# A delta-rule loop written out as one fixed order on four engines, with a smaller state and a rewritten k eviction

## The chip, the cores and the metric

The kernel runs on one core of one Trainium2 chip. The metric is device time in microseconds (us). The kernel before took 1830.32 us in the median of 3 runs (1828.99 to 1832.56).

## The reference

A two-layer decoder trunk on 1024 tokens of width 1024, all in float32. Layer 0 mixes the tokens with RWKV-7's delta rule, layer 1 with differential attention; each is followed by a gated per-layer embedding (PLE), and a norm ends it. The part that the change touches is layer 0's mixer. For each of 16 heads, `k`, `r`, `v`, a decay `w` and a rate `a` come from projections, and the state (64 x 64 per head) runs through the tokens:

```
kk = (k * k_k) / norm ;  b = kk * a ;  k = k * (1 + (a - 1) * k_a)
def step(state, (r_t, w_t, k_t, v_t, kk_t, b_t)):
    sa    = state @ kk_t
    state = state * w_t - sa b_t^T + v_t k_t^T
    y_t   = state @ r_t
y = groupnorm(y) * ln_w + ln_b + sum(r * k * r_k) * v      # the sum is the "bonus"
h = x + (y * silu(gate)) @ w_out
```

## The kernel before

The sequence is cut into 16 chunks of 64 tokens (`for c in range(NCH)`). Products with the large weights are three fp32r matmuls of high and low parts each (lines 75 to 77, `mm3`); products of the recurrence are plain float32, and each of those shows as two records of the trace. The 16 heads stand in two groups `st` of 8, four pairs `p_` with two halves `h`; a pair fills 128 partitions.

A chunk is a chain. `chain_x` multiplies the state with the chunk's `kk` and `r` (line 855) and adds masked products with `v` (line 864); ScalarE copies the result `x` (line 878), and GpSimd multiplies the state by the chunk's decay into `spl` (line 875). `chain_u` multiplies by a triangular inverse (line 890), and VectorE scales it into `vu` (line 895). `chain_s` makes the state's addition (line 906), which VectorE adds to `spl` (line 910), and finishes the outputs (line 916), which ScalarE copies into `y` (line 923). In the state of before a pair's two 64 x 64 blocks lie on the diagonal of a 128 x 128 tile, with zeros beside them.

Beside the chain runs other work. For each group of the next chunk, `stage1` loads `kkr` and `kb`, multiplies `kb` by the decay on GpSimd (`kbp`, line 171), transposes it (line 175) into `kbn` (ScalarE, line 176), makes the mask products `pm` (line 185) and masks them on VectorE (line 188), and makes the bonus: two passes on GpSimd (lines 157 and 158), two transposes (line 162), two sums on VectorE (line 166). Each 128 tokens (two chunks) have their norm (`norm`, `norm2`, lines 953 to 970), a transpose of `y` (line 981, `turn`), a gating (line 984) with the split into `gh` on ScalarE (line 71) and `gl` on VectorE (line 72), and the output projection of 48 matmuls (`op`, `mms`), which VectorE adds to the residual (line 997). The first four chunks instead carry layer 1's PLE projections (`pps`) and the loading and splitting of the eight rows of the output weight (`wo_row`).

The order is made by the tile scheduler: the chain's matmuls stand under `high_priority`, the rest lies in lists (`later`, `ahead`) that `weave` mixes by cost and `fill` hands out in budgets between the steps of the chain. SyncE issues the loads.

Before the loop, `ev_k` (line 423 on) takes each of 16 pieces of the k projection out of PSUM and makes `k * (1 + (a - 1) k_a)`, `kk` and `b`, scaled by exponentials of the summed decay (`pinv`, `ep`); `kst` (line 464) transposes the squares of `kk` for its norm, one piece later.

Of the kernel before, what the change touches and what calls it, by code (L numbers as in the profile page):

```python
# [11 lines left out]
F32 = mybir.dt.float32  # L12
# [4 lines left out]
ALU = mybir.AluOpType  # L17
# [20 lines left out]
def trunk(ctx: ExitStack, tc: tile.TileContext, A, out):  # L38
    nc = tc.nc
    V, S, G, T = nc.vector, nc.scalar, nc.gpsimd, nc.tensor  # L40
# [95 lines left out]
    units = {}  # L136

    def stage1(st, c):
# [15 lines left out]

        def bonus():
            pr = early["co"].tile([P, 4, L], F32, tag="prod", name="pr" + u, bufs=1)
            G.tensor_tensor(out=pr, in0=kkr[:, :, oc], in1=kb[:, :, oc], op=ALU.mult)
            G.tensor_tensor(out=pr, in0=pr, in1=vec["r_k"][:, j0:j0 + 4].unsqueeze(2).to_broadcast([P, 4, L]),
                            op=ALU.mult)
            pt = ps1[0].tile([P, 2, P], F32, tag=ps1[1], name="prt" + u, bufs=2)  # L160
            for p_ in range(2):
                T.transpose(pt[:, p_], pr[:, 2 * p_:2 * p_ + 2].rearrange("p a l -> p (a l)"), ident)
            po = (c % 2) * 64
            bo = bon[po:po + 64, c // 2, st * 8:st * 8 + 8].rearrange("p (a b h) -> p a b h", a=2, b=2)
            for b in range(2):
# [12 lines left out]
        def mh():
# [12 lines left out]
        return [(load, 0), (turn, 430), (mh, 850), (bonus, 430)]  # L191

    with NB("ab") as ab, NP("psab") as pp:
# [12 lines left out]
        G.tensor_scalar(out=hka1, in0=vec["k_a"], scalar1=-0.5, scalar2=1.0, op0=ALU.mult, op1=ALU.add)  # L206
# [127 lines left out]
        with NB("cpool") as cpl:  # L334
# [82 lines left out]
            with NB("kr") as a3:  # L417
# [5 lines left out]
                def ev_k(j, hf, ps):  # L423
# [11 lines left out]
                    t = tmp(f"kt{j}{hf}")  # L435
# [380 lines left out]
    with NB("d") as d, NP("psco") as pp:  # L816
# [26 lines left out]
        def chain_x(c):  # L843
# [3 lines left out]
            if c + 1 < NCH:  # L847
                vload(c + 1)
# [786 lines left out]
```

## Time and profile before

| | |
|---|---|
| median of the runs | 1830.32 us |
| profiled execution | 1828.3 us |
| its span | 1826.5 us |
| TensorE busy | 1684.7 us, 92% of the span |
| VectorE busy | 1350.9 us, 74% |
| ScalarE busy | 760.4 us, 42% |
| GpSimd busy | 634.5 us, 35% |
| mean granted clock of TensorE | 0.963 |

The busy shares are means over stages with different limits. The chunks run from 588.2 us, where chunk 0's state product starts, to 911.2 us, where chunk 15's outputs have been copied: 323.0 us in all. Chunks 4, 6, 8, 10, 12 and 14 start at 666.7, 704.5, 745.2, 785.1, 829.7 and 868.8 us. The k eviction lies between 125 and 250 us.

### The profile page before, as it was taken

How to read it: one execution, taken by the hardware profiler on the slowest of the kernel's cores; microseconds unless marked ns; L12 is line 12 of the kernel's file. 1: busy time of each engine (PE TensorE's matmuls, PEld its weight loads, DVE VectorE, ACT ScalarE, POOL GpSimd, SP SyncE). 2: the span in 40 equal slices, each digit the busy share in tenths (PEclk: the TensorE clock that was granted, in tenths of full speed). 3: DMA queues.
4: the chain of work that ended last, by engine and by line, in shares of the span. 5: the costliest groups of instructions: out<-in, count | busy, mean ns of one | idle time of the engine just before them, and what ended most of it. 6: DMA issues, size and time to landing. Idle time of an engine off the chain costs nothing.

```text
span 1826.5 us, 30473 instructions
## 1 busy us (share of the span) xinstructions
PE 1684.7 (92%) x11320; PEld 1397.6 (77%) x11320; DVE 1350.9 (74%) x3083; ACT 760.4 (42%) x1594; POOL 634.5 (35%) x705
## 2 busy tenths in 40 slices
PE   6899999898897988898899999899999999999998
PEld 5677778887676877777678878788888888777786
DVE  7878954698994687666766747887877878856665
ACT  6566543346344332223333434444444444544332
POOL 4436644224324355455310333323323323311200
PEclk9999999998998989999999999999999999999999
DMA  7125444434225534444243411101101101431121
GB/s 267 41 61 166 129 106 109 125 102 119 73 67 186 186 127 127 122 129 131 97 172 128 132 51 39 54 7 56 56 7 56 53 10 56 154 99 34 58 93 69
DMA packets 164401, 175.97 MB, mean 96 GB/s; under 512 B 74845, under 2 KB 127837, under 8 KB 164254
## 3 DMA queue, kind: packets, MB, share of 16 engines
q1 hardware_dynamic: 161950, 169.84, 30.2%
q10 hardware_dynamic: 2304, 4.20, 0.6%
q8 instruction: 89, 1.46, 0.4%
q14 instruction: 58, 0.48, 0.1%
HBM read 124.19 MB, written 49.81 MB: 95 GB/s over the span
## 4 chain that ended last, share of the span: by engine, by line
PE 51%; DVE 10%; ACT 2%; issue 1%; DMA 0%; POOL 0%; ACTq 0%; DVEq 0%
PE qkv L75 6%; PE qkv L76 6%; PE qkv L77 6%; PE av L1359 3%; PE sc L1319 2%; PE sc L1320 2%; PE fg L75 2%; PE fg L76 2%; PE fg L77 2%; PE op L75 2%; PE op L77 2%; PE op L76 2%; PE do L75 1%; PE pg L76 1%; PE pg L77 1%; PE do L76 1%
## 5 line engine op out<-in xcount | busy, mean ns | idle before, releaser
L1329 ACT ACTIVATE e<-sc,mx 128x256 f32<-128x256 f32 (+7 forms) x128 | 94.0, 738 | 111.0 <-DVE mx L1326 60.0
L1273 POOL TENSOR_TENSOR rp<-rp,rq 128x128 f32<-128x128 f32 x64 | 34.8, 543 | 237.6 <-DVE rq L1268 189.7
L1359 PE MATMUL av<-vh,aT 128*128 128x128 f32 x576 | 81.1, 280 | 6.3 <-DVE aT L1355 6.3
L1359 PEld LDWEIGHTS av<-vh,aT 128*128 128x128 f32 x576 | 75.6, 195 | 12.8 <-DVE aT L1355 8.9
L1325 DVE TENSOR_REDUCE mxs<-sc 128x1 f32<-128x128 f32 (+6 forms) x112 | 74.2, 682 | 0.5
L1319 PE MATMUL sc<-k,q 128*128 128x512 f32 (+2 forms) x192 | 71.5, 379 | 2.2 <-ACT e L1329 2.2
L229 DVE SCALAR_TENSOR_TENSOR xmt<-hT,cB,xmt 128x512 f32<-128x512 f32 x64 | 63.5, 1012 | 6.6 <-ACT xmt L228 6.3
L1320 PE MATMUL sc<-k,q 128*128 128x512 f32 (+2 forms) x192 | 64.8, 348 | 0.0
L1361 ACT ACTIVATE o<-av,r 128x128 f32<-128x128 f32 x64 | 23.5, 367 | 88.4 <-PE av L1359 88.4
L875 POOL TENSOR_TENSOR spl<-state,plast 64x256 f32<-64x256 f32 x60 | 41.4, 690 | 49.6 <-DVE state L910 42.7
L1341 DVE SCALAR_TENSOR_TENSOR e<-e,r,e 128x128 f32<-128x128 f32 (+3 forms) x64 | 56.5, 883 | 1.2
L560 DVE TENSOR_TENSOR tb<-tb,tm 128x31 f32<-128x31 f32 (+15 forms) x124 | 53.9, 435 | 3.6
L558 DVE TENSOR_TENSOR tm<-tb,nb 128x31 f32<-128x31 f32 (+15 forms) x124 | 53.9, 434 | 3.6
L188 DVE TENSOR_TENSOR m<-pm,mmask 128x512 f32<-128x512 f32 x64 | 41.1, 682 | 20.0 <-PE pm L185 19.7
L1301 POOL CAST q<-q 64x128 fp32r<-64x128 f32 x128 | 38.5, 302 | 49.4 <-PE sc L1320 45.6
L1267 DVE TENSOR_TENSOR rp<-qkv,rc 128x256 f32<-128x256 f32 x64 | 27.1, 423 | 38.3 <-PE qkv L77 30.1
L1292 POOL CAST k<-k 64x256 fp32r<-64x256 f32 x64 | 26.1, 408 | 83.7 <-ACT k L1290 82.5
L185 PE MATMUL pm<-kkr,kb 64*128 64x128 f32 x512 | 50.8, 307 | 3.1 <-ACT kbn L176 2.2
L1355 DVE COPY aT<-at 128x512 f32<-128x512 f32 (+2 forms) x96 | 52.0, 550 | 1.1 <-PE at L1353 0.4
L185 PEld LDWEIGHTS pm<-kkr,kb 64*128 64x128 f32 x512 | 40.4, 203 | 12.9 <-issue 6.0
L1353 PE MATMUL at<-ident,e 128*128 128x128 f32 x288 | 47.4, 277 | 2.8 <-DVE e L1341 2.3
L923 ACT COPY y<-xy 64x512 f32<-64x512 f32 x32 | 18.6, 580 | 71.4 <-PE xy L916 71.0
(1180 smaller groups left out, 6001.5 us busy)
## 6 DMA issues: line engine op xcount, KB each, us to landing
pp_d<-ppo SPq DMA_DIRECT2D x32, 256.0 KB, 2.3
kb_d<-kb SPq DMA_DIRECT2D x16, 512.0 KB, 2.6
kkr<-kkr_d SPq DMA_DIRECT2D x32, 256.0 KB, 3.2
kb<-kb_d SPq DMA_DIRECT2D x32, 256.0 KB, 3.3
x<-in_x SPq DMA_DIRECT2D x8, 512.0 KB, 5.5
kkr_d<-ep SPq DMA_DIRECT2D x16, 256.0 KB, 2.6
kkr_d<-rt SPq DMA_DIRECT2D x16, 256.0 KB, 2.6
bb<-kb_d SPq DMA_DIRECT2D x32, 128.0 KB, 2.6
```

The lines of the kernel that those rows point to most:

```text
L75: T.matmul(ps, lhsT=ah, rhs=bh, start=start, stop=False)
L76: T.matmul(ps, lhsT=ah, rhs=bl, start=False, stop=False)
L77: T.matmul(ps, lhsT=al, rhs=bh, start=False, stop=stop)
L185: ms.append(T.matmul(pm[h][:, p_], lhsT=kb[hs, p_], rhs=kkr[hs, p_], start=True, stop=True))
L229: V.scalar_tensor_tensor(out=t, in0=hT[:, kt, half(hf)], scalar=cB[:, g, kt:kt + 1], in1=t, op0=ALU.mult, op1=ALU.add)
L558: V.tensor_tensor(out=tv, in0=tb[:, j:j + 1, 0:w].to_broadcast([P, n, w]), in1=nb[:, j + 1:32, j:j + 1].to_broadcast([P, n, w]), op=ALU.mult)
L1319: T.matmul(ps[:, b0:b1], lhsT=q1[:, m, ts_], rhs=k1[:, m, b0:b1], start=True, stop=False)
L1320: T.matmul(ps[:, b0:b1], lhsT=q0[i % 2][:, m], rhs=k2[:, b0:b1], start=False, stop=True)
L1325: V.tensor_reduce(out=seed, in_=ps[:, 0:n - P], axis=AX.X, op=ALU.min)
L1329: S.activation(e[:, 0:n], ps[:, 0:n], AF.Exp, scale=-1.0, bias=mx, accum_out=l_[:, m:m + 1])
L1341: V.scalar_tensor_tensor(out=es[0][:, 0:n], in0=es[1][:, 0:n], scalar=r[:, 1:2], in1=es[0][:, 0:n], op0=ALU.mult, op1=ALU.add)
L1359: T.matmul(po, lhsT=aT[kb // 4][:, kb % 4], rhs=c["vh"][:, kb], start=(kb == 0), stop=(kb == i))
```

## The change

In the loop every instruction of TensorE, VectorE, ScalarE and GpSimd keeps the order in which the code issues it (a wrapper calls `keep_in_program_order` while `pin` is set; SyncE's is left to the scheduler), and that order is written out, step by step, in the place of the lists and budgets. The steps of a tile are cut finer (`norm`, `squares`, `bonus_v`, `sums`, `roots`, `scaled`, `added`, `turn`, `turned`, `m0`, `m1`, `squares1`), and likewise those of `stage1`.

The state becomes one tile of 128 x 512 without the zero blocks. Its product takes 16 matmuls of 64 rows, 128 weight columns and 64 moving columns a chunk, in the place of 8 of 128 x 128 x 128; `spl` is one instruction on GpSimd in the place of four, and so is the state's sum on VectorE. The chain's `xy` is one tile of two PSUM banks.

The bonus multiplies `r * k` once on GpSimd and sums on TensorE, against a matrix `rk2` of two columns (8 matmuls a group), and two copies on ScalarE; the transposes and the sums on VectorE are gone. Of the masks one half stays on VectorE; the other is copied by ScalarE and then multiplied in place by GpSimd. In the k eviction VectorE has three passes in the place of five, ScalarE two more, GpSimd one less. The early gate rows are prepared at the end of chunk 13, and the last tiles' pieces (`t6`, `t7`) behind the loop stand in another order: all 48 projection matmuls of tile 6 now lie there, where 12 stood in chunk 15.

Counted over the program, VectorE goes from 3085 to 2912 instructions, ScalarE from 1363 to 1459, GpSimd from 710 to 652; the attention layer's order is the same.

```diff
+        def g(*a, **k):
+            r = f(*a, **k)
+            if self.pin:
+                tc.keep_in_program_order(r)
+            return r
...
-            for h in range(2):
-                V.tensor_tensor(out=m[:, h], in0=pm[h],
-                                in1=early["mmask"][:, st:st + 1].to_broadcast([P, 4, P]), op=ALU.mult)
+            mask = early["mmask"][:, st:st + 1].to_broadcast([P, 4, P])
+            S.copy(m[:, 1], pm[1])
+            G.tensor_tensor(out=m[:, 1], in0=m[:, 1], in1=mask, op=ALU.mult)
+            V.tensor_tensor(out=m[:, 0], in0=pm[0], in1=mask, op=ALU.mult)
...
+                    ms.append(T.matmul(pt[64 * s_:64 * s_ + 64, p_], lhsT=pr_[:, s_, p_],
+                                       rhs=early["rk2"][:, 4 * s_ + p_], start=True, stop=True))
...
-                    t = tmp(f"kt{j}{hf}")
-                    V.tensor_scalar(out=t, in0=a, scalar1=hka[:, jj], scalar2=hka1[:, jj],
-                                    op0=ALU.mult, op1=ALU.add)
-                    V.tensor_tensor(out=t, in0=ps3, in1=t, op=ALU.mult)
...
+                    V.tensor_tensor(out=q, in0=ps3, in1=pinv, op=ALU.mult)
...
+                    V.scalar_tensor_tensor(out=a, in0=a, scalar=1.0, in1=q, op0=ALU.add, op1=ALU.mult)
...
-                    V.tensor_scalar(out=a, in0=a, scalar1=-0.5, scalar2=-0.5, op0=ALU.mult, op1=ALU.add)
...
-                    V.tensor_tensor(out=kb[:, :, 1 - px], in0=t, in1=pinv, op=ALU.mult)
-                    V.tensor_tensor(out=a, in0=kk, in1=a, op=ALU.mult)
-                    G.tensor_tensor(out=kb[:, :, px], in0=a, in1=pinv, op=ALU.mult)
+                    S.activation(q, q, AF.Copy, scale=hka1[:, jj])
+                    V.scalar_tensor_tensor(out=kb[:, :, 1 - px], in0=a, scalar=hka[:, jj], in1=q,
+                                           op0=ALU.mult, op1=ALU.add)
+                    S.activation(kb[:, :, px], a, AF.Copy, scale=hkk[:, jj])
...
-                    ms += [T.matmul(px_[st][:, p_].rearrange("p h l -> p (h l)"), lhsT=kkr[:, p_],
-                                    rhs=state[st][:, p_], start=(p_ == 0), stop=False, skip_group_check=True)
-                           for p_ in range(4)]
+                            ms.append(T.matmul(px[:, h, st, p_], lhsT=kkr[half_(h), p_], rhs=state[half_(h), st, p_],
+                                               start=(st == 0 and p_ == 0), stop=False, skip_group_check=True))
...
+                V.tensor_tensor(out=state, in0=pS, in1=spl.rearrange("p (s j) l -> p s j l", s=2), op=ALU.add)
...
+            chain_x(c)
+            unit("decayed", 0)
+            if pj and not odd:
+                pj["turned"]()
+                pj["turn"](1)
...
+            more()
+            unit("mh", 0)
+            if pj and not odd:
+                pj["turned"]()
...
+            chain_u(c)
...
+            chain_s(c)
...
+            if c == 3:
+                more(9)
+                for kt in (2, 3, 6, 7):
+                    wo_row(kt)
...
+            more(2)
+            unit("turn", 1)
+            if w and odd:
+                w["added"]()
+                w["turn"](0)
+            more(9)
```

`unit` issues a step of `stage1` for the next chunk, `w` is the tile whose norm is under way, `pj` the one in projection, and `more` issues six projection matmuls at a time.

The first place is the start of an even chunk. On TensorE in chunk 6, between `x`'s products and the next, before (`ytr` is the transpose of `y`, `op` the projection, `u` the triangular product, `kbt` the transpose of `kbp`):

```order
L864 MATMUL xy_6_6867<-vu_6627,m_6_6621 64x64
L162 MATMUL prt_6_6839<-ident,pr_6_6836 128x128 x2
L981 MATMUL ytr_6844<-ident,y_5924 128x128 x4
L75 MATMUL op_6912<-rwo0h,gh_6783 128x512
L76 MATMUL op_6912<-rwo0l,gh_6783 128x512
L75 MATMUL op_7116<-rwo0h,gh_6783 128x512
L76 MATMUL op_7116<-rwo0l,gh_6783 128x512
L890 MATMUL u_6_6946<-x_6893,ti_2685 64x64
L175 MATMUL kbt_7_6906<-ident,kbp_7_6904 128x128 x4
```

and now (`pm` are the mask products of chunk 7):

```order
L50 MATMUL xy_6838<-vu_6616,m_6_6605 64x64
L50 MATMUL ytr_6880<-ident,y_5924 128x128 x4
L50 MATMUL op_6889<-rwo0h,gh_6800 128x512
L50 MATMUL op_6889<-rwo0l,gh_6800 128x512
L50 MATMUL op_6889<-rwo0h,gl_6801 128x512
L50 MATMUL op_6889<-rwo1h,gh_6800 128x512
L50 MATMUL op_6889<-rwo1l,gh_6800 128x512
L50 MATMUL op_6889<-rwo1h,gl_6801 128x512
L50 MATMUL pm_7_6897<-kkr_7_6823,kb_7_6824 128x128
L50 MATMUL pm_7_6896<-kkr_7_6823,kb_7_6824 128x128
```

The state and mask products that make `x` stand ahead of all these rows. Before, the products with `gl` (`op<-rwo0h,gl`) come only after `u`; now the third matmul behind the transpose needs it.

On ScalarE, which makes `gh`, from which VectorE makes `gl`, the same stretch in chunk 8 stood before as

```order
L957 ACTIVATE ysq_7491<-y_6855 128x1024
L71 ACTIVATE gh_7224<-sg_7042 128x512
L878 COPY x_7334<-xy_8_7313 64x512
L878 COPY x_7334<-xy_8_7308 64x512
L176 COPY kbn_9_7300<-kbt_9_7347 128x512
L71 ACTIVATE gh_7224<-sg_7042 128x512
L923 COPY y_7296<-xy_8_7313 64x512
L923 COPY y_7296<-xy_8_7308 64x512
L176 COPY kbn_9_7304<-kbt_9_7416 128x512
L1001 ACTIVATE h1sq_7634,ss_5440<-xr_7044 128x1024
```

and stands now as

```order
L50 COPY x_7312<-xy_7277 64x512 x2
L50 ACTIVATE gh_7239<-sg_6935 128x512
L50 COPY m_9_7264<-pm_9_7336 128x512
L50 ACTIVATE gh_7239<-sg_6935 128x512
L50 ACTIVATE h1sq_7350,ss_5430<-xr_6498 128x1024
L50 COPY kbn_9_7265<-kbt_9_7378 128x512
L50 COPY m_9_7268<-pm_9_7393 128x512
L50 COPY y_7261<-xy_7277 64x2x4x64 x2
L50 ACTIVATE ysq_7448<-y_6822 128x1024
L50 COPY kbn_9_7269<-kbt_9_7464 128x512
L50 COPY bon<-prt_9_7470 64x8 x2
```

The first `gh` was ahead of the copies of `x`; now it is behind them, and the copy of a mask half stands ahead of the second.

The second place is the end of an odd chunk, on VectorE. Before, around chunk 6 (`vu` the scaled triangular product, `m` the masks, `xr` the residual):

```order
L895 TENSOR_TENSOR vu_6627<-u_6_6946,rn 64x512
L966 TENSOR_TENSOR y_6414<-y_6414,gst_7046 128x1024
L895 TENSOR_TENSOR vu_6627<-u_6_6945,rn 64x512
L188 TENSOR_TENSOR m_7_6858<-pm_7_6920,mmask 128x512
L188 TENSOR_TENSOR m_7_6858<-pm_7_6919,mmask 128x512
L970 TENSOR_TENSOR y_6414<-y_6414,vn_7040 128x1024
L910 TENSOR_TENSOR state_5478<-s_6_6988,spl_6_6894 64x4x64 x2
L910 TENSOR_TENSOR state_5480<-s_6_6999,spl_6_6898 64x4x64 x2
L166 TENSOR_REDUCE bon<-prt_7_6940 64x2x2 x2
L997 TENSOR_TENSOR xr_6603<-op_6912,xr_6603 128x512
```

and now, at the end of chunk 5 and the start of chunk 6 (`sg` is the gating behind the transpose):

```order
L50 TENSOR_TENSOR m_6_6605<-pm_6_6678,mmask 128x512
L50 TENSOR_TENSOR vu_6398<-u_5_6691,rn 64x512
L50 TENSOR_TENSOR vu_6398<-u_5_6692,rn 64x512
L50 TENSOR_TENSOR y_5924<-y_5924,gst_6527 128x1024
L50 TENSOR_TENSOR m_6_6609<-pm_6_6727,mmask 128x512
L50 TENSOR_TENSOR state<-s_6743,spl_6652 128x512
L50 TENSOR_TENSOR xr_6033<-op_6671,xr_6033 128x512
L50 TENSOR_TENSOR y_5924<-y_5924,vn_6494 128x1024
L50 SCALAR_TENSOR_TENSOR sg_6496<-ytr_6802,vecs,sg_6496 128x128 x4
L50 TENSOR_TENSOR gl_6801<-sg_6496,gh_6800 128x512
L50 SCALAR_TENSOR_TENSOR sg_6496<-ytr_6880,vecs,sg_6496 128x128 x4
```

The residual sum `xr<-op` needs the last projection matmul of the chunk; now the sum `y<-y,vn`, which the next transposes read, stands behind it.

## Rows read from the trace of the kernel before

**Rows 1.** The page of the whole run: busy time of each engine, share of the span.

```profile
PE 1684.7 (92%) x11320; PEld 1397.6 (77%) x11320; DVE 1350.9 (74%) x3083; ACT 760.4 (42%) x1594; POOL 634.5 (35%) x705
```

**Rows 2.** Windows: stretch, length, busy time (instructions) of each engine, granted clock, DMA.

```profile
210.00:250.00 40.00, 32.65 (x131) 25.27 (x130) 38.84 (x47) 23.09 (x37) 24.43 (x16) 0.91 0.36 103
588.20:666.70 78.50, 72.23 (x831) 61.57 (x830) 51.74 (x87) 24.29 (x38) 35.70 (x39) 0.88 0.52 169
666.70:785.10 118.40, 105.17 (x1298) 88.65 (x1296) 85.28 (x174) 30.67 (x51) 61.22 (x67) 0.97 0.40 121
868.80:911.20 42.40, 33.86 (x389) 28.08 (x387) 32.90 (x68) 14.49 (x22) 16.88 (x14) 0.95 0.30 99
```

**Rows 3.** TensorE in chunk 11: start, length, line, output<-inputs, records [idle before <-releaser].

```profile
802.13 1.15 PE L906 MATMUL s<-vu,kbn 128*64 128x64 f32 x32
...
804.15 0.93 PE L185 MATMUL pm<-kkr,kb 64*128 64x128 f32 x10
...
805.35 0.39 PE L76 MATMUL op<-rwo4l,gh 128*128 128x512 f32 x1
...
805.58 0.40 PE L77 MATMUL op<-rwo4h,gl 128*128 128x512 f32 x1
...
808.55 1.95 PE L855 MATMUL xy<-state,kkr 128*128 128x128 f32 x16
...
810.34 0.38 PE L162 MATMUL prt<-ident,pr 128*128 128x128 f32 x2
```

**Rows 4.** The same view of the one product with 32-column weights, in the lead-in.

```profile
430.24 2.05 PE L593 MATMUL pg<-prhs,pairs 64*64 64x32 f32 x64 [1.28 <-ACT prhs L574]
```

**Rows 5.** Groups of the loop: VectorE, ScalarE, GpSimd; busy, mean ns of one | idle.

```profile
L188 DVE TENSOR_TENSOR m<-pm,mmask 128x512 f32<-128x512 f32 x60 | 38.6, 682 | 16.7 <-PE pm L185 16.4
...
L984 DVE SCALAR_TENSOR_TENSOR sg<-ytr,vecs,sg 128x128 f32<-128x128 f32 x56 | 15.9, 344 | 1.2 <-PE ytr L981 0.8
...
L72 DVE TENSOR_TENSOR gl<-sg,gh 128x512 fp32r<-128x512 f32 x14 | 11.0, 789 | 0.0
...
L970 DVE TENSOR_TENSOR y<-y,vn 128x1024 f32<-128x1024 f32 x7 | 9.5, 1354 | 4.2 <-POOL y L967 4.1
...
L997 DVE TENSOR_TENSOR xr<-op,xr 128x512 f32<-128x512 f32 x12 | 8.3, 690 | 13.4 <-PE op L77 13.3
...
L878 ACT COPY x<-xy 64x512 f32<-64x512 f32 x32 | 18.5, 580 | 25.5 <-PE xy L864 24.7
...
L71 ACT ACTIVATE gh<-sg 128x512 fp32r<-128x512 f32 x14 | 8.8, 630 | 20.9 <-DVE sg L984 20.9
...
L171 POOL TENSOR_TENSOR kbp<-kb,plast 128x512 f32<-128x512 f32 x30 | 32.3, 1078 | 9.6 <-PE kbt L175 8.4 <-DMA kb<-kb_d 1.2
```

**Rows 6.** TensorE where it waits before a chunk's transposes and after the early gate rows.

```profile
790.75 1.11 PE L981 MATMUL ytr<-ident,y 128*128 128x128 f32 x4 [1.88 <-DVE m L188]
...
829.70 3.78 PE L855 MATMUL xy<-state,kkr 128*128 128x128 f32 x16 [5.19 <-ACT y L923]
```

**Rows 7.** Waits of 180 to 310 us: who for whom, total, times, longest.

```profile
PE kst L464 <- ACT kks L454: 7.1, 2, 3.8
```

**Rows 8.** VectorE groups of 190 to 300 us, the k eviction's five and line 229.

```profile
L229 DVE SCALAR_TENSOR_TENSOR xmt<-hT,cB,xmt 128x512 f32<-128x512 f32 x16 | 18.2, 1164 | 0.0
...
L436 DVE TENSOR_SCALAR kt<-as,hka,hka 128x512 f32<-128x512 f32 x5 | 6.3, 1263 | 1.3 <-ACT as L434 1.1 <-DVE as L448 0.2
...
L447 DVE TENSOR_TENSOR kb<-kt,pi 128x512 f32<-128x512 f32 x5 | 6.1, 1214 | 0.0
...
L448 DVE TENSOR_TENSOR as<-kk,as 128x512 f32<-128x512 f32 x5 | 4.0, 793 | 0.0
...
L438 DVE TENSOR_TENSOR kt<-d,kt 128x512 f32<-128x512 f32 x5 | 3.4, 684 | 0.2
...
L445 DVE TENSOR_SCALAR as<-as 128x512 f32<-128x512 f32 x5 | 3.3, 664 | 0.0
```

**Rows 9.** VectorE's sum of line 970 behind the loop, where it took longest.

```profile
934.35 3.40 DVE L970 TENSOR_TENSOR y<-y,vn 128x1024 f32<-128x1024 f32 x1 [2.30 <-POOL y L967]
```

More of the change, by code (lines that the diff above doesn't have):

```diff
@@ L859, in chain_x, with chain_u @@
+            ctx_c[0] = (vu2, px, spl, x)
+        def chain_u(c):
+            vu2, px, spl, x = ctx_c[0]
+            ti = tis[c // 4]
+            pu = [pp.tile([P, 4, 2, L], F32, tag="us", name=f"u{st}_{c}", bufs=2) for st in range(2)]
+            ms = []
+            if True:
                 for p_ in range(4):
@@ L1058, in trunk @@
         for c in range(NCH):
-            if c % 2 == 0:
+            i, odd = (c - 2) // 2, c % 2
+            if not odd:
                 D1[c // 2] = {"y": dt_("y", f"y{c // 2}", 3)}
-            for at_, pc in ahead:
-                if at_ == c:
-                    later[c].extend(pc)
-            work = weave(stage1(0, c + 1) + stage1(1, c + 1) if c + 1 < NCH else [], later[c])
-            tot = sum(x[1] for x in work)
-            def fill(budget):
-                while work and budget > 0:
-                    f, cost = work.pop(0)
-                    f()
-                    budget -= cost
@@ new lines, in trunk @@
+            if c == 2:
+                wo_row(5)
+            chain_u(c)
+            if w:
+                w["scaled" if odd else "load"]()
+            unit("turn", 0)
+            unit("decayed", 1)
+            more()
+            unit("mh", 1)
+            if w and not odd:
+                w["norm"]()
+            unit("pr", 0, 1)
+            if c == 1:
+                wo_row(1)
+            chain_s(c)
+            if c == 1:
+                wo_row(4)
+            if c == 3:
+                more(9)
+                for kt in (2, 3, 6, 7):
+                    wo_row(kt)
@@ L1093, in trunk @@
+            if w and not odd:
+                w["squares"]()
+                w["bonus_v"]()
+            more(2)
+            unit("turn", 1)
+            if w and odd:
+                w["added"]()
+                w["turn"](0)
+            more(9)
+            unit("bonus", 1)
+            if c == 12:
+                early_raw()
+            if c == 13:
+                early_row(0)
+                early_row(1)
+        for e in engines:
+            e.pin = False
         co_cm.__exit__(None, None, None)
@@ L1176, in trunk @@
         mms2(0)
-        run(t7)
-        run(later[NCH + 2])
+        for hf in range(2):
+            t7["turn"](hf)
+            t7["turned"]()
+        run(t7["m0"] + t7["m1"])
+        t7["squares1"]()
         pre2(1)
```

308 lines of the change are left out of this document (160 added, 148 removed).

## The prediction, made before the changed kernel was run

> **What bounds the kernel now.** I read the page's shares first. TensorE is busy 92% of the span, VectorE 74%, and the other two under half [rows 1]; so a change pays where TensorE waits or runs at a lower clock, and nowhere else. Next come the windows of the two stages that the change touches [rows 2]. In the k eviction (210 to 250 us) it is VectorE that is full, 38.84 of 40 us, while TensorE idles 7.35 us at a granted clock of 0.91. In the loop (chunks 4 to 9, 666.7 to 785.1 us) VectorE has a third of its time free; TensorE is busy 105.2 of 118.4 us, so it idles 13.2 us in three pairs of chunks, 4.4 a pair. The reader is to see that the loop is a chain of short handovers around a nearly full TensorE, and that the last pair (868.8 to 911.2 us) is longer, 42.4 us with 8.5 idle, although chunk 15 prepares no next one.
>
> Third is TensorE's own timeline for the price of each step [rows 3], and fourth what it waits for [rows 6]: the transposes of `y` wait for VectorE, which is in the norm of the tile when the mask products come; and after a wait the same work costs more. The state product takes 1.95 us in chunk 11 [rows 3] and 3.78 behind the wait of 5.19 us [rows 6], so that the granted clock is at the lower of its levels, 1.2 GHz, there. A wait of 1.88 us is followed by it too: four transposes take 1.11 us [rows 6], where two take 0.38 at the full clock [rows 3].
>
> **The change, part by part.** The sum is against the profiled execution, 1828.3 us; the median of the runs lies 2.0 above that, and I add this at the end.
>
> State product. Before, 16 records in 1.79 us (808.55 to 810.34), 112 ns each [rows 3]. Now 32 records of 64 rows, 128 weight columns and 64 moving columns, the halves of the array in turn. The nearest row is the mask product, also of 64 rows and 128 weight columns in turn: 10 records start within 0.93 us less the about 0.3 us of the last, 70 ns each [rows 3]. A floor is the product of 64 rows with 32 columns, 64 records in 2.05 us, 32 ns each [rows 4]. So it costs 1.0 us (32 x 32), 2.2 (32 x 70) or 3.6 us (32 x 112, were each load as dear as a full one); I take 2.0, since half the columns move, as against the mask product's 128: +0.2 a chunk. Against that the written order lets whole products stand together where the old one cut them (the transposes inside `u`, a projection matmul inside `pm`): two cuts fewer a chunk, at an estimated 0.1 us each (from the first mask record at 804.15 to the second projection matmul at 805.35 there are 1.20 us; 10 x 0.07 and one matmul of 0.23 leave 0.27 for the change of form and the pipeline's end) [rows 3]. The two cancel; the bounds over 15 chunks with a state are -14 and +27.
>
> The Trainium skill ("TensorE: Matmul & The Clock Gate", section "LDWEIGHTS (loading the stationary operand)") says that a load's time goes by its columns and not by its rows, so that a 64-row weight of 128 columns loads no faster than a 128-row one; by its figure of 107 ns for 128 columns the product would be estimated at 3.4 us. The trace does not agree for products whose halves alternate: the mask product's 70 ns a record is below that [rows 3].
>
> The bonus. Two transposes (0.38 us [rows 3]) become 16 records of 64 weight columns and two moving ones; at the 32 ns of the nearest row [rows 4] 0.5 us. Nothing, then, on TensorE; the ends, 0.2 us a unit either way, are small beside those above. VectorE is relieved of two reductions a unit, GpSimd of one pass, ScalarE gains two short copies: none is the loop's bound.
>
> Masks. VectorE's pass on one half (0.68 us [rows 5]) becomes ScalarE's copy (0.58, as `x`'s) and GpSimd's product (1.08, as line 171's [rows 5]). The mask is read by the next chunk's products, half a chunk later or more; what hides it is that distance. Without it the step would cost 1.0 us a unit. Likewise `spl`: one GpSimd instruction of 128x512 (about 1.08) and one sum of 0.7 on VectorE, in the place of four and four.
>
> The even chunk's wait. On TensorE the transpose of `y` (about 0.6 us, twice the 0.38 for two) and two projection matmuls (0.23 us apart [rows 3]) follow `x`'s products, and the third needs `gl`. On ScalarE `gh` is now behind both copies of `x`: 2 x 0.58 + 0.63, then `gl` on VectorE 0.79 [rows 5], with about 0.3 for three handovers 2.9 us. TensorE has 1.06 us of work: it waits 1.8 us. Behind `gl` VectorE also has four gatings of 0.34 [rows 5] before a mask half; the mask products' second set waits a little for the buffer, which I count at 0.2.
>
> The odd chunk's wait. VectorE's `xr<-op` (0.69) waits for the last projection matmul, `y<-y,vn` (1.35) stands behind it [rows 5], and then come the transposes of `y`: 2.0 us and 0.2 of handovers, against TensorE's four transposes of `kbp`, 0.6. It waits 1.6 us. Behind `y<-y,vn` on VectorE are the gatings, `gl` and the next masks: all of the next chunk, and their readers come after the transposes anyway. The state's sum, which the next state product needs, stands ahead of both and has over 2 us left.
>
> Together 3.6 us a pair; before, 4.4 a pair. I expect a fall of the clock behind one of them as before, and small handovers of some tenths that I can't see in an order. So ordinary pairs stay at 39.4 us, the mean of chunks 4 to 9 (118.4 / 3 = 39.5 [rows 2]) and 12 to 13 (39.1): 0. Bounds: both waits halved and no fall of the clock, -2 a pair; and the slower rival below.
>
> Chunks 0 to 3. Before, 78.5 us with 6.3 idle at a clock of 0.88 [rows 2]. Now four rows of the output weight stand on VectorE ahead of `y<-y,vn` at the end of chunk 3. Each is a pass over 128x1024 with two inputs, 1.35 us by line 970's row [rows 5]: 4 x 1.35 + 1.35 = 6.8 us, in which TensorE has a few transposes. That eats what a smoother start may give. 0, with -6 (all the idle time gone) and +8 as ends.
>
> Early gate rows. They cost 5.19 us of waiting and 1.8 of clock at 829.70 [rows 6], because ScalarE waited for their loads ahead of `y`'s copies. The loads are now a chunk earlier than their use, and the four ScalarE instructions stand behind `y`'s copies; they delay the next `x`, by about 1.7 us (four of some 1.1 us, less the state product and mask products beside them). 5.2 - 1.7 = 3.5, the clock falling once as before: -3.5; ends -7 and 0.
>
> The last pair. Two chunks without chunk 15's preparation: TensorE's busy 35.1 us of a pair (105.2 / 3), less two mask products of 16 records (10 took 0.93, so 2 x 1.4), two units' transposes (2 x 0.6 and 2 x 0.4 for the bonus), the state's addition 1.15 [rows 3], is 29.2; with 4.4 idle 33.6. Before, 42.4 [rows 2]: -8.8. But 12 projection matmuls went behind the loop (12 x 0.23 = 2.8), and two gate rows, which were made in chunk 15, are made there, 1.2 us late by one ScalarE pass: +4. Net -4.8, ends -9 and +2.
>
> k eviction. VectorE's five passes cost 1.26 + 0.68 + 1.21 + 0.79 + 0.66 = 4.6 us a piece [rows 8]. The three that follow are one like line 448 (0.8) and two like line 229 (1.16 [rows 8]): 3.1. That is 1.5 us less on the engine that is full, times 16 pieces 24 us; GpSimd loses a pass, ScalarE gains two at about 0.6, and is busy 23 of 40 us [rows 2]. TensorE can only gain its idle time: 7.35 us, of which 7.1 is the `kst` transposes waiting for ScalarE's squares [rows 7], which wait for VectorE, and up to 3.6 of clock (9% of 40 us). What is late next is ScalarE's chain of `q`, squares and `kb`. I take -7, the wait without the clock; ends 0 and -11.
>
> Sum: 0 (products) + 0 (pairs) + 0 (chunks 0 to 3) - 3.5 - 4.8 - 7 = -15.3; 1828.3 - 15.3 + 2.0 = 1815 us.
>
> **Rivals.** *More gain*: the state product at the 32 ns floor, -0.9 a chunk, -14 us; the two waits halved and no fall of the clock behind them, -2 a pair over 7 pairs, -14 us: 1787. For it: the halves' loads overlap in the mask product, and the written order's waits are each below 2 us. Against it: the 1.88 us wait was followed by the lower clock [rows 6].
>
> *No gain*: the last pair keeps its 42 us since nothing but the order fills it, and the eviction's wait passes from VectorE to ScalarE: 1827 to 1831. Against it is the size of VectorE's relief.
>
> *Slower*: in the written order a late VectorE instruction holds all behind it, where the old order had put other work ahead. The place is `y<-y,vn` at the end of odd chunks: it took 3.40 us once, behind the loop [rows 9], against a mean of 1.35 [rows 5]; GpSimd is now given the masks and `bonus_v` in that stretch. Were it 2.0 longer in each pair and a further fall of the clock followed (1.8, as 3.78 against 1.95), a pair costs +3.8, seven pairs +27: 1842. It decides from 15.3 / 7 = 2.2 us a pair. For it: the wait stands in every pair, with nothing behind it on TensorE. Against it: inside the loop GpSimd ran as densely before, and the mean was 1.35.
>
> The Trainium skill ("GPSIMD Engine Reference", section "1. Specifications") says that GpSimd's memory interfaces are shared with VectorE, with contention for VectorE instructions of two inputs; line 970's 3.40 us [rows 9] would fit it, though the row does not show that it is the cause.
>
> The dear loads of the state product are a second way to slower: +27, 1842 as well.
>
> **How the numbers follow.** About 0.2%, 3.7 us, is what a measurement here can tell from no change. Forecast 0.47, with an own range of 1798 to 1826; more gain 0.24; no gain 0.10; slower by the wait 0.15, by the loads 0.04. The range runs from 1778 (the second case with some of the eviction's clock) to 1845 (the slower cases with a little more). Faster than 1826.6: 0.24 + 0.45 of the forecast's case, and 0.01 of the third: 0.70; slower than 1834: 0.19 and 0.01 of the forecast's tail: 0.20; the same: 0.10.
>
> **What would show it.** The state product in 32 records of 60 to 70 ns. TensorE idle about 1.8 us before the first `gl` product of even chunks and 1.6 before the transposes at the end of odd ones, pairs of 39 to 40 us, the last of about 34. No wait above 4 us between chunks 11 and 14. In the k eviction `kst` waiting less than 2 us and VectorE below 85% busy. I am wrong if ordinary pairs differ from 39.4 by more than 2 us either way, or if the wait at the end of chunk 3 exceeds 8 us.

## The result, and the profile after

The changed kernel takes 1818.28 us in the median of 4 runs (1816.69 to 1821.92), the one before 1830.51 beside it: a ratio of 0.9935, with a 95% interval of 0.9916 to 0.9955. The forecast was 1815 us. The profiled execution took 1819.65 us; it is 8.65 us below the profiled one of before, where the medians differ by 12.2. The comparison by stages below is one of single executions, so its lines together miss 3.6 us of the difference.

In the changed kernel's profile all of the four engines' instructions carry line 50, that of the wrapper; its rows are told apart by their tiles. The page's first part answers to [rows 1]:

```profile
span 1817.8 us, 31112 instructions
...
PE 1683.5 (93%) x11768; PEld 1393.4 (77%) x11768; DVE 1268.2 (70%) x2910; ACT 799.4 (44%) x1690; POOL 608.4 (33%) x647
```

VectorE lost 83 us of work, TensorE 1.2. The windows that answer to [rows 2] are the k eviction, chunks 0 to 3, chunks 4 to 9 and chunks 14 to 15, and after them the stretch from chunk 15's end to the last projection matmul, whole and its first 30 us (length, busy time of PE, PEld, DVE, ACT, POOL, granted clock, DMA):

```profile
210.00:250.00 40.00, 36.95 (x158) 28.96 (x157) 33.53 (x41) 24.79 (x41) 21.13 (x12) 0.96 0.48 129
575.10:656.80 81.70, 69.47 (x970) 58.44 (x968) 43.17 (x59) 33.29 (x58) 45.53 (x34) 0.90 0.63 194
656.80:773.80 117.00, 107.70 (x1468) 89.75 (x1466) 66.60 (x119) 38.37 (x73) 60.96 (x48) 0.92 0.38 115
848.30:882.00 33.70, 27.96 (x392) 23.11 (x389) 19.44 (x35) 18.36 (x28) 17.58 (x11) 0.93 0.34 110
882.00:935.10 53.10, 44.25 (x181) 34.81 (x180) 32.91 (x63) 13.85 (x19) 11.58 (x5) 0.85 0.47 159
882.00:912.00 30.00, 21.40 (x76) 16.07 (x74) 27.10 (x50) 11.20 (x15) 11.58 (x5) 0.73 0.64 221
```

The reader is to see three things: VectorE no longer fills the eviction (33.5 of 40 us); chunks 4 to 9 are only 1.4 us shorter than before, though VectorE's work in them fell by 19 us; and the last pair is 8.7 us shorter, but the stretch behind it runs at a clock of 0.85. In chunks 4 to 9 two things cancel: TensorE idles 9.3 us where it idled 13.2, but it is at its lower clock for 19.4 us and not for 6.8; 12.6 of the 19.4 are what is left of a fall that began in the wait at the end of chunk 3.

The whole difference, cut at the same products in both traces (us, profiled executions):

| stretch | before | after | difference | forecast |
|---|---|---|---|---|
| start to the product behind the k eviction (`pb`) | 325.9 | 319.0 | -6.9 | -7 |
| from there to chunk 0 | 262.3 | 256.1 | -6.2 | 0 |
| chunks 0 to 3 | 78.5 | 81.6 | +3.1 | 0 (-6 to +8) |
| chunks 4 to 9 | 118.4 | 117.0 | -1.4 | 0 |
| chunks 10 to 13, with the early gate rows | 83.7 | 74.5 | -9.2 | -3.5 |
| chunks 14 and 15 | 42.4 | 33.7 | -8.7 | -8.8 |
| to the last projection matmul | 40.5 | 53.1 | +12.6 | +4 |
| PLE products | 89.0 | 89.4 | +0.4 | 0 |
| first 114 us of the attention | 107.9 | 114.1 | +6.2 | 0 |
| the rest | 677.9 | 679.2 | +1.3 | 0 |

TensorE's timeline around the end of chunk 3 and in chunks 5 and 6 (start, length, output<-inputs, records [idle before <-releaser]):

```profile
596.38 2.00 PE L50 MATMUL xy<-state,kkr 64*128 64x64 f32 x32
...
654.78 1.09 PE L50 MATMUL ytr<-ident,y 128*128 128x128 f32 x4 [9.57 <-DVE y L50]
...
696.24 0.63 PE L50 MATMUL ytr<-ident,y 128*128 128x128 f32 x4 [1.57 <-DVE y L50]
...
702.42 0.50 PE L50 MATMUL op<-rwo0h,gh 128*128 128x512 f32 x1 [1.40 <-ACT gh L50]
```

The state product takes 2.00 us, 62 ns a record, as forecast (2.0). The odd chunk's wait is 1.57 us, forecast 1.6. The even chunk's is 1.40, forecast 1.8: TensorE waits two matmuls earlier than forecast, for `gh` and not for `gl`. And the end of chunk 3 has the one long wait, 9.57 us, whose cause stands on VectorE (the last rows of the output weight, and then the tile's sum). VectorE waits there too, 2.45 and 1.12 us, for ScalarE, which makes the rows' high parts:

```profile
645.73 1.76 DVE L50 TENSOR_TENSOR rwo2l<-rwo2r,rwo2h 128x1024 fp32r<-128x1024 f32 x1 [2.45 <-ACT rwo2h L50]
...
652.28 1.22 DVE L50 TENSOR_TENSOR rwo7l<-rwo7r,rwo7h 128x1024 fp32r<-128x1024 f32 x1 [1.12 <-ACT rwo7h L50]
653.42 1.22 DVE L50 TENSOR_TENSOR y<-y,vn 128x1024 f32<-128x1024 f32 x1
```

Behind chunk 15 the lead is lost. VectorE and GpSimd there, and TensorE's waits:

```profile
879.48 2.36 POOL L50 TENSOR_TENSOR pwg<-pwg05r,pwg 128x1024 fp32r<-128x1024 f32 x1 [9.05 <-ACT pwg L50]
879.61 3.31 DVE L50 TENSOR_TENSOR y<-y,gst 128x1024 f32<-128x1024 f32 x1
...
882.84 1.21 DVE L50 TENSOR_REDUCE gst<-y 128x16 f32<-128x1024 f32 x1
...
885.45 1.23 DVE L50 TENSOR_TENSOR y<-y,gst 128x1024 f32<-128x1024 f32 x1
...
887.31 1.22 DVE L50 TENSOR_TENSOR y<-y,vn 128x1024 f32<-128x1024 f32 x1
...
888.67 1.94 PE L50 MATMUL ytr<-ident,y 128*128 128x128 f32 x8 [3.35 <-DVE y L50]
...
891.54 2.35 POOL L50 TENSOR_TENSOR pwg<-pwg03r,pwg 128x1024 fp32r<-128x1024 f32 x1 [6.16 <-ACT pwg L50]
...
891.67 2.25 DVE L50 TENSOR_SCALAR rn<-rn 128x6 int32<-128x6 int32 x1
892.98 0.79 PE L50 MATMUL op<-rwo0h,gh 128*128 128x512 f32 x1 [2.37 <-ACT gh L50]
896.80 0.79 PE L50 MATMUL op<-rwo0h,gl 128*128 128x512 f32 x1 [1.75 <-DVE gl L50]
```

An instruction of 128 x 6 elements took 2.25 us and ended at 893.92, with GpSimd's pass (893.89). The sum of 3.31 us takes 1.23 where no pass of GpSimd runs beside it; it ended 1.08 us after GpSimd's. So VectorE was held by GpSimd there. The rows at 882.84 and 885.45 belong to tile 7's norm; they stand ahead of tile 6's sum (887.31), for which TensorE's transposes wait. At the head of the attention the same is seen (VectorE alone; GpSimd splits weights from 1021.86 to 1028.94 without a break):

```profile
1022.19 2.07 DVE L50 SCALAR_TENSOR_TENSOR da6t<-da6r,da6m 128x1 f32<-128x1 f32 x1
1024.30 2.33 DVE L50 SCALAR_TENSOR_TENSOR da6r<-da6t,da6r 128x1 f32<-128x1 f32 x1
1026.67 2.82 DVE L50 TENSOR_SCALAR n2r<-h1b,da6r 128x1024 f32<-128x1024 f32 x1
```

One-column instructions that took 0.14 and 0.22 us just before take 2.07 and 2.33. The section on the change said that the attention's order is the same. It is not wholly so: in its first 30 us some rows of VectorE and TensorE changed places.

### The profile page after: what moved, and what is told of

It is laid out like the page before. It is cut to its first block, busy times and chain, and to the rows that moved or that the text cites. A ratio compares the mean times of both kernels' runs of the same rounds, so it can differ in the third digit from the quotient of the medians.

```text
span 1817.8 us, 31112 instructions
## 1 busy us (share of the span) xinstructions
PE 1683.5 (93%) x11768; PEld 1393.4 (77%) x11768; DVE 1268.2 (70%) x2910; ACT 799.4 (44%) x1690; POOL 608.4 (33%) x647
## 4 chain that ended last, share of the span: by engine, by line
PE 53%; DVE 7%; ACT 1%; DMA 1%; issue 1%; POOL 0%; SPq 0%; DVEq 0%; ACTq 0%; POOLq 0%
PE qkv L50 18%; PE fg L50 5%; PE do L50 4%; PE pg L50 4%; PE op L50 4%; PE sc L50 4%; PE av L50 3%; PE xy L50 2%; PE pm L50 2%; PE at L50 1%; DVE ost L50 1%; PE qkt L50 1%; DVE aT L50 1%; PE u L50 1%; PE s L50 1%
## 5 line engine op out<-in xcount | busy, mean ns | idle before, releaser
L50 POOL TENSOR_TENSOR rp<-rp,rq 128x128 f32<-128x128 f32 x128 | 61.8, 504 | 230.4 <-DVE rq L50 187.0
L50 PE MATMUL sc<-k,q 128*128 128x512 f32 (+2 forms) x384 | 88.7, 363 | 3.8 <-ACT e L50 2.2
L50 POOL TENSOR_TENSOR m<-m,mmask 128x512 f32<-128x512 f32 x32 | 41.9, 1311 | 112.3 <-ACT m L50 112.3
L50 PEld LDWEIGHTS sc<-k,q 128*128 128x128 f32 x384 | 63.2, 190 | 12.9 <-ACT e L50 3.0
L50 PE MATMUL pg<-pwg,ph 128*128 128x512 f32 x224 | 72.3, 401 | 0.2 <-ACT ph L50 0.2
L50 PE MATMUL do<-dwo,oh 128*128 128x512 f32 x224 | 71.7, 401 | 0.8 <-DVE h L50 0.5
L50 DVE SCALAR_TENSOR_TENSOR ost<-ost 128x2 f32<-128x2 f32 x192 | 47.4, 247 | 3.8
L50 DVE TENSOR_TENSOR m<-pm,mmask 128x512 f32<-128x512 f32 x32 | 22.1, 691 | 39.8 <-PE pm L50 37.5
```

The costliest lines, as they stand in the source:

```text
L50: r = f(*a, **k)
```

## The experiments

Medians are of 4 to 12 runs each; the kernel before, run beside them, lay between 1829.2 and 1830.3 us. Ratios are to that kernel. The changed kernel's own runs spread over 5 us, so a difference of 2 to 4 us from it is at the edge of what the runs can tell.

**1. The k eviction alone**, in the kernel before: the eviction's lines as in the diff above, nothing else.

> The kernel before with the rewritten k eviction alone. In the profile of the changed kernel the first product of the stage behind the eviction (pb) starts at 319.0 us, before at 325.9. Theory 1 (VectorE was the bound there): this kernel gains the same 7 us by itself, so 1823 to 1824 us, with pb at 319 and the kst transposes waiting under 2 us. Theory 2 (the 7 us come from another part, or are lost again in the loop, whose chunks wait for VectorE anyway): pb at 319 but 1828 to 1831 us.

Measured: 1830.37 us, ratio 1.0005 (0.9995 to 1.0015): no gain. `pb` starts at 318.8 us, so the stage did gain its 7 us, and chunk 0 began 6.6 us earlier. But chunks 10 to 13 took 89.3 us, before 83.7, and by the end of the loop the lead was gone. The loop's code is that of before; its order is not: of TensorE's 3378 instructions between chunk 0 and the loop's end 2446 stand in the same sequence. So the scheduler planned the loop anew once the eviction changed. The second theory's time is right, for another reason than it gave: the lead was lost under a new order, and where the order is held the same 7 us reach the end (experiment 5).

**2. No order kept**, in the changed kernel:

```diff
-        for e in engines:
-            e.pin = True
```

> The changed kernel with its instructions left to the scheduler, no order kept. In the changed kernel ordinary pairs of chunks take 37.2 to 38.8 us, before 37.8 to 40.7. Theory 1 (the written order makes the loop's gain): pairs go back to 39 to 40 us or above, and the whole is 10 to 20 us slower than the changed kernel, 1828 to 1838 us. Theory 2 (the smaller state and the passes taken off VectorE make it): pairs stay at 37 to 39 us and the whole at 1814 to 1822 us.

Measured: 1832.67 us, ratio 1.002 (1.001 to 1.003); pairs of 40.4 to 43.3 us. The first theory: the written order is worth 14.4 us, more than the whole gain. Left to the scheduler, the smaller state, the new eviction and the work taken from VectorE together bring nothing. What each of them is worth under the kept order was tested for the eviction alone (experiment 5).

**3. The order kept behind the loop too**, up to the end of tile 6's projection (the loop that clears `pin` moves there).

> The changed kernel with the order kept on until the projection of tile 6 behind the loop is done. In the changed kernel the stretch from the end of chunk 15 to tile 7's projection takes 41.9 us, before 29.2; of the 12.7 us more 4 were foreseen. Theory 1 (the gate rows and tile 7's norm, which no order holds, move ahead of tile 6's sum on VectorE, so that TensorE waits 3.35 + 2.37 + 1.75 us and runs at half clock): held back, they leave the stretch at 33 to 36 us and the whole at 1810 to 1814 us. Theory 2 (GpSimd's passes hold VectorE there, whatever the order): 40 to 43 us and 1817 to 1820 us.

Measured: 1817.79 us, ratio 0.9942 (0.9927 to 0.9956), not to be told from the changed kernel and in the second theory's range. The waits before tile 6 fell from 7.5 to 3.4 us (2.00 and 1.44), and one of 7.39 came for tile 7's sum:

```profile
912.74 1.51 PE L50 MATMUL ytr<-ident,y 128*128 128x128 f32 x6 [7.39 <-DVE y L50]
```

**4. The gate rows' low halves on VectorE.**

```diff
-        EG = (G, G)
+        EG = (None, None)
-        GE = (None, None, None, G, None, G, None, G)
+        GE = (None,) * 8
```

> The changed kernel with the low halves of the gate rows made by one pass on VectorE (1.28 us) and not on GpSimd (2.4 us); in the profile of the changed kernel VectorE's instructions of two inputs or of small size end together with such GpSimd passes (3.31 us for a pass of 1.22, 2.25 us for one of 0.15). Theory 1 (GpSimd's passes hold VectorE): the stretch behind the loop shortens from 41.9 to 36 to 39 us, the whole to 1812 to 1816 us. Theory 2 (the order in which VectorE takes the work decides): no gain or a loss of 1 to 4 us, since VectorE has five passes more.

Measured: 1814.63 us, ratio 0.992 (0.9907 to 0.9933), in the first theory's range; the interval overlaps a little with the changed kernel's. The same two places on VectorE, and the last where GpSimd still has a pass:

```profile
876.81 1.38 DVE L50 TENSOR_TENSOR vu<-u,rn 64x512 f32<-64x512 f32 x2
878.23 1.23 DVE L50 TENSOR_TENSOR y<-y,gst 128x1024 f32<-128x1024 f32 x1
...
889.39 0.16 DVE L50 TENSOR_SCALAR rn<-ss 128x6 f32<-128x6 f32 x1
...
892.52 1.90 POOL L50 TENSOR_TENSOR vn<-vn,bon 128x1024 f32<-128x1024 f32 x1 [10.55 <-DMA vn<-v_d]
892.66 1.78 DVE L50 TENSOR_SCALAR rn<-rn 128x6 int32<-128x6 int32 x1
```

The sum takes 1.23 us again, and the small instruction is held only where GpSimd runs (till 894.44 and 894.42). From the end of chunk 15 to the attention's first product there are 139.5 us, in the changed kernel 142.5, before 129.4: 3 of the 13 us come back.

**5. The old k eviction** in the changed kernel.

> The changed kernel with the old k eviction put back. The rewritten eviction alone gave the kernel before nothing (1830.4 against 1829.3 us), though its chunks then began 6.6 us earlier: the scheduler had ordered the loop anew. Theory 1 (the 7 us last where the loop's order is held): without them 1823 to 1827 us, pb at 325 to 327 us, chunks 4 to 14 as in the changed kernel within 3 us. Theory 2 (a later stage takes back whatever the eviction gives): 1816 to 1820 us.

Measured: 1826.16 us, ratio 0.9976 (0.9966 to 0.9986): 7.9 us slower than the changed kernel. `pb` at 326.8; from the start of chunk 4 to that of chunk 14 it takes 189.4 us, there 191.5. The first theory: where the order is held, the eviction's 7 us reach the end. The waits of `kst` for ScalarE are there in the two kernels with the old eviction (3.3 and 3.8 us before, 3.4 and 3.7 here), and none of over 1 us is left in the others.

**6. The first two heads' low halves on VectorE.**

```diff
-                    split(hh, ll, dw0[k4], (G, G, V, G)[k4])
+                    split(hh, ll, dw0[k4], V)
-                        wload2(ph + 1, i - 2, G)
+                        wload2(ph + 1, i - 2, V if ph == 0 else G)
```

> The changed kernel with the low halves of the first two heads' attention weights (seven rows) made by VectorE (1.21 us each) and not by GpSimd (2.4 us). At the head of the attention the changed kernel lost 6 to 7 us of its lead on the one before (17.0 us ahead in the last PLE products, 10.1 forty us later). Theory 1 (GpSimd's passes hold VectorE, whose small instructions took 2.07 and 2.33 us beside them): the loss falls to 0 to 3 us, the whole to 1812 to 1816 us. Theory 2 (the loss is the order of the first products, or VectorE's own load): loss of 5 us or more, 1817 to 1823 us.

Measured: 1816.02 us (1808.86 to 1817.67), ratio 0.991 (0.989 to 0.9929). The lead on the kernel before is 14.4 us in the last PLE products and 14.4 eighty us later; in the changed kernel it goes from 16.1 to 10.0. The first theory, in the place. In the whole the gain is 2.3 us, and the interval overlaps with the changed kernel's; in the profiled execution this kernel came to the attention 1.6 us later than the changed one, in stages whose code is the same.

**7. The rows of the output weight split.**

```diff
+            if c == 4:
+                wo_row(6)
+                wo_row(7)
...
-                for kt in (2, 3, 6, 7):
-                    wo_row(kt)
...
+            if c == 3:
+                wo_row(2)
+                wo_row(3)
```

> The changed kernel with the last four rows of the output weight taken behind the tile's sum: two at the end of chunk 3, two in chunk 4. In the changed kernel TensorE waits 9.57 us there, and runs 20.5 us at half clock behind it. Theory 1 (the rows on VectorE ahead of the sum are the wait): it falls under 3 us, and chunk 6 starts 8 to 14 us earlier: 1805 to 1812 us. Theory 2 (the wait moves to the products of chunk 4, whose low halves stand behind the rows on VectorE): a wait of 4 to 8 us there, and 1813 to 1819 us.

Measured: 1812.94 us, ratio 0.9906 (0.9892 to 0.992), 5.3 us faster, between the two theories' ranges. The wait of 9.57 us fell to 0.52 and chunk 4 began 10 us earlier, but half of it was given back in chunks 4 and 5 (45.9 us, there 40.6), by a wait of the second theory's kind, though on ScalarE, at the lower clock:

```profile
666.10 1.74 PE L50 MATMUL pm<-kkr,kb 64*128 64x128 f32 x13 [3.24 <-ACT kbn L50]
```

**8. Gate rows on VectorE, and tile 7's norm first**, with the order kept (experiment 4, and behind the loop `t7`'s steps with two gate rows between them ahead of `t6["m0"]`).

> The changed kernel with the gate rows' low halves on VectorE, and the order kept behind the loop with tile 7's norm ahead of tile 6's projection. With the rows on VectorE alone it was 1814.6 us, with the order kept alone 1817.8: there TensorE's waits before tile 6 fell from 7.5 to 3.4 us, but it waited 7.39 us for tile 7's sum. Theory 1 (both waits are VectorE's, and go with the right order): the stretch from chunk 15's end to tile 7's first product takes 32 to 36 us and not 41.9, the whole 1806 to 1812 us. Theory 2 (VectorE's work behind chunk 15 is as long as TensorE's, so that a wait stays wherever it is put): 38 to 42 us and 1813 to 1818 us.

Measured: 1819.22 us, ratio 0.9937 (0.9923 to 0.9951). Tile 7's transposes came 33.0 us behind chunk 15, as the first theory had it, but the time did not follow and lies above both ranges: waits of 3.55 us for `ph` and 3.58 for tile 7's sum stand in the PLE products, and to the attention there are 145.5 us. That speaks for the second theory: a wait stayed wherever it was put.

**9. Two steps of the written order moved.**

```diff
+            if pj and not odd:
+                pj["turned"]()
             chain_x(c)
             unit("decayed", 0)
             if pj and not odd:
-                pj["turned"]()
                 pj["turn"](1)
...
+            if w and odd:
+                w["added"]()
             more(2)
             unit("turn", 1)
             if w and odd:
-                w["added"]()
                 w["turn"](0)
```

> The changed kernel with two steps of its written order moved: on even chunks the first split of the gated tile stands ahead of the state product and so ahead of the copies of x on ScalarE, and on odd chunks the sum y<-y,vn stands ahead of the residual sum that waits for the last projection matmul. The two waits a pair that the prediction named, 1.40 and 1.57 us in chunks 6 and 5 of the changed kernel, are then without their cause. Theory 1 (they are all that TensorE waits for in a pair, and the falls of its clock follow them): both go under 0.3 us, ordinary pairs take 33 to 35 us and not 37 to 39, the whole 1796 to 1806 us. Theory 2 (the next engine in line takes their place, GpSimd's product of y in odd chunks above all, or the clock falls all the same): pairs of 36 to 38 us, 1810 to 1818 us.

Measured: 1803.87 us, ratio 0.9861 (0.9847 to 0.9874), 14.4 us faster than the changed kernel by two moved lines, in the first theory's range; which of the two brings how much was not tested. Chunks 6 to 11 of this kernel, and the sum on VectorE in chunk 5 with what is around it:

```profile
697.23:800.59 103.36, 101.47 (x1466) 86.70 (x1464) 70.30 (x120) 38.72 (x75) 61.76 (x49) 0.97 0.50 149
```

```profile
692.05 2.06 DVE L50 TENSOR_TENSOR y<-y,vn 128x1024 f32<-128x1024 f32 x1 [0.24 <-POOL y L50]
694.95 0.69 DVE L50 TENSOR_TENSOR xr<-op,xr 128x512 f32<-128x512 f32 x1 [0.84 <-PE op L50]
```

Three pairs take 103.4 us, in the changed kernel 113.7: 3.5 a pair less. TensorE idles 1.9 us in the three, there 9.5, which is 2.5 a pair; the rest is the clock, at its lower level for 6.8 us and not 10.2. These 6.8 us fall in chunks 6 to 9, though TensorE waited for nothing longer than 0.33 us there; with the clock full, chunks 10 and 11 took 33.4 us. The sum is even slower here (2.06 us, beside GpSimd), but nothing waits for it.

**10. Experiments 4, 6, 7 and 9 together.**

> The changed kernel with four edits together: the gate rows' and the first two heads' low halves on VectorE, the four rows of the output weight split between chunks 3 and 4, and the two steps moved. Alone the first three gave -3.6, -2.3 and -5.3 us against the changed kernel's 1818.3. Theory 1 (they take away waits in different places and add up): with the moved steps' -12 to -20, 1787 to 1797 us. Theory 2 (a lead in the loop is lost again at the head of the attention, where VectorE and the loads set the pace): the loop ends 25 us or more earlier than the changed kernel's, the whole gains less than 18, 1800 to 1808 us.

Measured: 1781.49 us (1778.69 to 1787.46), ratio 0.9741 (0.9725 to 0.9758): 36.8 us below the changed kernel, where the four gains alone add up to 25.6, and below both theories' ranges. Chunks 6 to 11:

```profile
693.70:794.00 100.30, 98.40 (x1468) 83.93 (x1466) 68.47 (x120) 39.13 (x76) 61.89 (x49) 1.00 0.53 161
```

The clock is full throughout; over the whole trace TensorE is at its lower clock for 118 us, in the changed kernel for 150, and in experiments 4, 6, 7 and 9 for 150, 155, 157 and 147. If work takes twice as long at the lower clock, 32 us less of it give back 16 at most (an estimate); the sum of the parts lacks 11. So the clock can account for it. That each part alone left waits which kept the clock falling is a likely reading, but not shown: the clock also fell in experiment 9 where no such wait was left.

**11. No order kept, the chain under high priority** as in the kernel before (experiment 2 with `with tc.high_priority():` around the chain's matmuls).

> The changed kernel left to the scheduler, as in the second experiment (1832.7 us), but with the chain's matmuls under high priority as in the kernel before. Theory 1 (keeping the order is what pays, since VectorE and ScalarE too must take the work in it): 1826 to 1834 us, pairs of 40 us or more. Theory 2 (the second experiment was slow for want of the priority): pairs of 37 to 39 us, 1814 to 1822 us.

Measured: 1888.04 us, ratio 1.0325 (1.0311 to 1.0339): neither number; it is 55 us slower than without the priority. TensorE's waits between 640 and 930 us (who for whom, total, times, longest):

```profile
PE ytr L50 <- DVE sg L50: 33.4, 6, 5.9
PE xy L50 <- DVE m L50: 13.8, 11, 1.9
```

The direction is the first theory's. Six times TensorE waits 4.6 to 5.9 us for VectorE's gating. That the priority put chain products ahead of work which would have covered VectorE's part is my reading of it, and was not tested by itself.

**12. Experiment 10 with the tail of experiment 8.**

> The four edits together (1781.5 us), and behind the loop the order kept with tile 7's norm ahead of tile 6's projection. With the four edits TensorE still waits 3.58 us for vu in chunk 15, 2.70 and 2.36 us before tile 6's products, and runs 13.6 us at half clock there. With this tail in the changed kernel the stretch behind chunk 15 took 34.4 us and not 41.9, but the loss came back as waits of 3.55 and 3.58 us. Theory 1 (a VectorE order that fits makes the tail shorter): 1775 to 1780 us. Theory 2 (VectorE has as much to do there as TensorE, whatever the order): 1780 to 1786 us.

Measured: 1779.17 us (1777.82 to 1782.7), ratio 0.9733 (0.972 to 0.9746): the fastest kernel here, though the interval doesn't part it from experiment 10. The time is the first theory's, but the tail did not get shorter: in the profiled executions chunk 15's outputs end 6.2 us earlier, where no gate row stands ahead of `vu` and its wait of 3.58 us is gone, and the stretch to the attention is 3.3 us longer.

## Why the prediction was right, point by point

The time lay in the likeliest case, and the mechanism held in the loop: TensorE's work unchanged, two short waits a pair of about the sizes that were named, in those places or two matmuls from them, the last pair shorter by 8.7 (forecast 8.8), the eviction's 7 us, which experiments 1 and 5 put to the eviction alone. That the sum came out within 3.3 us was partly luck, since errors of more than that cancelled:

- "Net -4.8" for the last pair and the tail. The tail was mis-sized: +12.6 and not +4. The count of projection matmuls behind the loop is about right (13 more in the trace, 5 of tile 6 and 8 of tile 5, where 12 of tile 6 were counted; the 8 had been counted in the last pair, so some 1.8 us of its 8.7, by 0.23 each, only moved behind it), but they were priced as TensorE's work alone. What I left out is that instructions outside the kept order move ahead of the kept ones (the gate rows and tile 7's norm stand before tile 6's sum on VectorE), and that GpSimd's passes hold VectorE. Experiments 3 and 8 show that the order alone doesn't mend it, 4 that GpSimd's part is about 3 us. For the rest, VectorE is the busier engine in the first 30 us there, 27.1 us against TensorE's 21.4, the time it was held included; which share of that could be hidden is open.
- The head of the attention was counted at nothing, since its order ends the same. It lost 6.2 us, and experiment 6 shows that GpSimd's splits beside VectorE are the cause (nothing lost without them).
- Chunk 0 began 6.2 us earlier than the eviction accounts for. TensorE had waited 6.12 us for GpSimd's bonus passes before chunk 0; the wait is 0.91 now, which is 5.2 of the 6.2. I had priced those passes in the loop, where they are hidden, and not before it.
- The early gate rows: chunks 10 to 13 gained 9.2, forecast 3.5. The wait of 5.19 us [rows 6] went; the new one I expected, 1.7, didn't show in that pair (37.4 us, before 44.6), and the other pair gained 1.9 as well.
- "Pairs of 39 to 40 us": 37.2 to 40.6. The 0 for chunks 4 to 9 came out because less idle time and more time at the lower clock cancelled.
- Both signs by which I had said I would be wrong were met, the first narrowly: the two pairs of chunks 10 to 13 took 37.35 and 37.19 us, 2.05 and 2.2 below 39.4, and the wait at the end of chunk 3 was 9.57 us, above the 8 that I had set. Experiment 7 shows the four rows to be its cause. I had priced them as VectorE's passes alone, at 6.8 us with the sum; VectorE's waits for ScalarE, 2.45 and 1.12 us, were left out.

*The slower rival* put GpSimd's hold on `y<-y,vn` in odd chunks. There the six sums took 1.21 us in the median and 2.12 at most, and in experiment 9 the sum takes 2.06 us in most odd chunks and is hidden. Its mechanism is real, in two other places. The Trainium skill ("GPSIMD Engine Reference", section "1. Specifications") says that GpSimd's memory interfaces are shared with VectorE, with contention for instructions in a two-port mode or with two inputs from memory; the traces agree for two inputs, with 3.31 us for the sum of 1.23, and with 0.68 to 0.69 us for passes that read PSUM beside GpSimd, as everywhere else. An instruction of one input was held too (`rn<-rn`, 2.25 us for 0.16); whether it ran in such a two-port mode, no run here shows.

*The dear loads*: 62 ns a record against 112. The records of the two halves' loads start 6 to 7 ns apart, and the next two about 105 ns later, so the halves' loads do overlap here. *More gain* had counted on 32 ns a record, which did not come, and on shorter waits, which experiment 9 then brought: what that rival had asked of the written order, two lines of it gave.

What I did not weigh at all is the largest number of the study: the order is worth 14.4 us (experiment 2), since the scheduler gave the other parts' gains away, as it did in experiment 1.

## What to carry to other kernels

Where a scheduler orders the work, a stage's gain shows only if the order behind it is held; compare the order of the two kernels in the stages that were not touched before crediting or blaming the edit. In a loop with a nearly full TensorE look for the short waits that come once a pass, and ask of each which instruction stands ahead of the one waited for on its engine: here two lines moved were worth 14.4 us, more than the whole change before them (12.2). A fall of the clock adds to the waits: 1.5 us a pair here, in some pairs and not in others of the same order. So gains of this size need not add up, and one profile of a pair is not enough to judge them.

## What the runs showed of the hardware

In these traces a pass of GpSimd on 128x1024 float32 (2.35 us) held most instructions of VectorE that start beside it and read no PSUM, until it ended: 2.25 us for one of 128 x 6, 2.07 and 2.33 us for ones of 128 x 1; one pass of 1.23 us took 3.31. Not every one was held: two of 128 x 1, int32 with one input, took 0.15 us each beside the pass that ran from 1018.54 to 1020.96 us. On VectorE the same split takes 1.22 to 1.28 us. The two kernels in which it was moved there were 3.7 and 2.3 us faster (1814.6 and 1816.0 against 1818.3 us), which is at the edge of the noise.

The granted clock fell in some pairs and not in others of the same order. Chunks 6 and 7 in the changed kernel, with 3.4 us at the lower clock (1.2 GHz), and in experiment 6, with none (the columns of the windows above):

```profile
697.36:735.05 37.69, 34.73 (x493) 28.80 (x489) 22.43 (x41) 13.02 (x25) 20.77 (x17) 0.95 0.41 128
```

```profile
696.57:732.71 36.14, 33.18 (x492) 27.72 (x489) 22.47 (x41) 13.02 (x25) 20.70 (x17) 1.00 0.44 132
```

TensorE's idle time is 2.96 us in both, in the two waits of 1.57 and 1.40 us, so the difference of 1.5 us is the clock's. Without these two waits a pair took 33.4 us wherever the clock stayed full (chunks 6 to 11 in experiment 10, 10 and 11 in experiment 9), but 35.0 in chunks 6 to 9 of experiment 9, where it fell twice behind no wait longer than 0.33 us. So the two waits alone do not decide whether it falls; what else does is open.
